# Hybrid decoder trunk on one core: one turn in each eighth chunk of the up-projection, mixer products back and forth from tile to tile, out-projection operands moved by 64 and 128 bytes

## The chip, the core and the metric

The kernel runs on one core of one Trainium2 chip. The metric is the device time of one execution in microseconds (us), lower is better; before the change three runs took 1076.39, 1076.42 and 1076.58 us, median 1076.42 us. One further execution was profiled. In what follows TensorE is PE, VectorE is DVE, ScalarE is ACT, GpSimd is POOL, and SP issues most of the transfers.

## What is computed

One decoder layer for 256 tokens of width 2048: a mixer that runs attention heads and a causal convolution side by side on one input projection, an output projection, and a gated MLP with a three-tap convolution. All in float32. Cut to what matters here:

```python
h = rms_norm(x, mix_norm_g[l])
proj = h @ w_in[l]
q, kv, gate_logits, conv_in = jnp.split(proj, splits, axis=-1)
...
attn = nsa_attention(q, kv, gates, rel_bias, cmp_pos[l], cmp_w1[l], cmp_w2[l])
conv = conformer_conv(conv_in, conv_w[l], conv_b[l], conv_ln_g[l], conv_ln_b[l])
x = x + jnp.concatenate([attn, conv], axis=-1) @ w_out[l]
h = rms_norm(x, ffn_norm_g[l])
x = x + conv_glu_ffn(h, w_up[l], ffn_conv_w[l], ffn_conv_b[l], w_down[l])
...
return rms_norm(x, final_norm_g)

def conv_glu_ffn(h, w_up, cw, cb, w_down):
    u = causal_depthwise_conv(h @ w_up, cw, cb)
    a, gate = jnp.split(u, 2, axis=-1)
    return (jax.nn.silu(gate) * a) @ w_down
```

`w_in` has 5680 columns, `w_up` 2 x 5632, `w_down` is 5632 x 2048. The four matrix products hold nearly all of the arithmetic.

## The kernel before

**Float32 in parts.** PE multiplies in the format fp32r, which keeps fewer bits than float32. So every operand is split into a high part (a rounded copy, made by ACT) and a low part (what is left, made by DVE or POOL), and a product x·w becomes three: high times high, high times low, low times high. The weights stream in chunks of 1 MB (`raw`, three buffers `wraw`); `w_split` makes `wh` and `wl` of each (three buffers each), two chunks ahead of PE. A weight buffer is free again when PE has used it.

**The stages,** in the order in which PE runs them:

- *The head*, to 24 us: the first three chunks of the mixer's projection, in pieces as their transfers land.
- *The mixer's projection*, to 250 us: 29 chunks through `tile_chunk` (L501). Each is one tile of 128 columns of `w_in` and 16 tiles of the sum over 2048, and each of the 16 goes through `mm3` (L252): three matmuls of 256 columns, with `wh` stationary twice and `wl` once. Between the chunks, and within them where `hook` says so, PE is given other matmuls: the compressed branch (`cmp_in`, L735), spreads of norms, the attention itself. After the 21st of the 29 chunks, six chunks for the values come with their own loops, then eight for the queries, with the attention's matmuls among them.
- *The out-projection*, to 353.5 us: `out_group` and `out_unit` (L1095, L1105), 125 calls of `mm_rows` (L269), each three matmuls of 512 columns. Here the activations are the stationary operand (`ma_h`, `ma_l` of the attention, `mc_h`, `mc_l` of the convolution, `ms_h`, `ms_l` of sums) and the weights stream.
- *The up-projection*, to 840 us: 88 chunks, numbered here 4m + 2·part + kh from 0 to 87 (loop at L1356). Each chunk has 16 steps j; a step is one `whole` (L1369: `wh` stationary, 512 columns, the high and the low activations side by side) and one `low` (L1381: `wl` stationary, 256 columns, the high activations). I call the two a pair. ACT and DVE work on the results meanwhile (`up_out`).
- *The down-projection*, to 1066 us, then the last norm and the stores.

**The order of the products.** PE takes its instructions in the order in which the program issues them, and two small tables set the order of matmuls that belong to one sum. They change no operand:

- `ROUNDS` (L49) orders the three products of `mm3`. It has four entries, taken in turn from chunk to chunk by `st["use"]`, and each entry has one order for every odd and one for every even call. Written with A for a matmul that has `wh` stationary and B for `wl`, two calls in a row are: order 0 AAB AAB, order 1 ABA ABA, order 2 BAA AAB, order 3 ABA AAB.
- `TURNS` (L50) orders steps 4 and 5 of an up-projection chunk, from chunk 4 on (`m > 0`), by the chunk's number modulo 5. Written with W for `whole` and L for `low`, the plain order of the two steps is W4 L4 W5 L5. Order 0 of the table is W4 L4 L5 W5, which I call the turn; 1 is W4 W5 L4 L5; 2 is the plain order; 3 is L4 L5 W4 W5; 4 is the plain order with W4 split into two matmuls of 256 columns (L1375). Chunks 0 to 3 are in plain order, but for other matmuls let into 0 and 1 (`between`).

**Where the tiles lie.** Tiles of one pool lie one behind the other in each partition's memory, so a longer tile moves all that follow it. In the built program the out-projection's stationary tiles `ma_h`, `ma_l`, `mc_h`, `mc_l`, `ms_h` all start 64 bytes past a multiple of 128, the high and the low parts alike. `wh` starts 64 bytes past such a multiple, `wl` and the activations `xt` on one.

Of the kernel before, what the change touches and what calls it, by code (L numbers as in the profile page):

```python
# [11 lines left out]
F32 = mybir.dt.float32  # L12
# [5 lines left out]
P = 128  # L18
T = 256
D = 2048  # L20
# [10 lines left out]
LINE = 16  # L31
# [12 lines left out]
CUTS = ((0, 1), (1, 2), (2, 4), (4, 5), (5, 6), (6, 8), (8, 10), (10, 12), (12, 14), (14, 16))  # L44
THIRD = {1: (0, 2), 2: (2, 4), 4: (4, 6), 5: (6, 8), 9: (8, 16)}
EARLY = 4


ROUNDS = (((0, 1, 2), (0, 1, 2)), ((0, 2, 1), (0, 2, 1)), ((0, 1, 2), (2, 1, 0)), ((0, 1, 2), (1, 2, 0)))  # L49
TURNS = (lambda w, s, l: ((w, 4), (l, 4), (l, 5), (w, 5)),  # L50
         lambda w, s, l: ((w, 4), (w, 5), (l, 4), (l, 5)),
         lambda w, s, l: ((w, 4), (l, 4), (w, 5), (l, 5)),
         lambda w, s, l: ((l, 4), (l, 5), (w, 4), (w, 5)),
         lambda w, s, l: ((s, 4), (l, 4), (w, 5), (l, 5)))


def head_of_slot(s):
# [5 lines left out]
def hybrid_trunk(ctx: ExitStack, tc: tile.TileContext, a: dict, out: bass.AP):  # L63
    nc = tc.nc
# [42 lines left out]
    st = {"dma": 3, "split": 3, "use": 0, "odd": 0}  # L107
# [4 lines left out]
    def w_dma():  # L112
        c = st["dma"]
        if c >= len(chunks):
            return
        st["dma"] += 1
        src, n = chunks[c]
        if c in kinds and c - down0 > 3 and (c - down0) % 4 == 3:
            raws[c] = late_pool[0].tile([P, CW], F32, name="wraw4", bufs=1)
        else:  # L120
            raws[c] = wpool.tile([P, CW], F32, name="wraw", bufs=NR)
        if c in far_sums:
            n = 1536
            nc.sync.dma_start(raws[c][:, n:], far_sums[c])
        if c == 4:
            nc.sync.dma_start(raws[c][:, :n // 2], src[:, :n // 2])
            halves.append(lambda: nc.sync.dma_start(raws[c][:, n // 2:], src[:, n // 2:]))
            return
        nc.sync.dma_start(raws[c][:, :n], src[:, :n])
# [101 lines left out]
    def w_next(cuts=1, ahead=LA):  # L231
        c = st["use"]
        st["use"] += 1
        w_pump()
        if st["split"] >= len(chunks):
            for f in lows:
                f()
            lows.clear()
        while st["split"] <= min(c + ahead, len(chunks) - 1):
            w_pump()  # L240
            w_split(cuts)
        if cuts == 1 or POOLED[0] <= st["split"] - 1 < POOLED[1]:
            w_pump()
        now = late[:]
        late.clear()
        if now:
            clock["dve"] = max(clock["dve"], clock["pe"])
        for f in now:
            f()
        return parts.pop(c)  # L250

    def mm3(ps, wh, wl, xh, xl, first, last):  # L252
        pairs = ((wh, xh), (wh, xl), (wl, xh))
        st["odd"] ^= 1
        for n, i in enumerate(ROUNDS[st["use"] % len(ROUNDS)][st["odd"]]):
            nc.tensor.matmul(ps, *pairs[i], start=first and n == 0, stop=last and n == 2)  # L256
        clock["pe"] += 0.36

    def mm_down(ps, xh, xl, wh, wl, first, last):
# [49 lines left out]
    xt_h, xt_l = [[xt[k // 4][:, k % 4, i] for k in range(KD)] for i in range(2)]  # L309


    with ExitStack() as mx:
        ap = mx.enter_context(tc.tile_pool(name="ap", bufs=1))
# [17 lines left out]

        ha = mixp.tile([P, KD + 8 * 512], F32, name="ha", tag="x2")
        raw2 = wpool.tile([P, CW], F32, name="wraw", bufs=NR)
        hb4 = [ap.tile([P, 4 * 512], F32, name=f"hb{i}", tag=tg) for i, tg in enumerate(("mah", "mal"))]
        mix_g = ha[:, :KD]
        heads, at = [], KD
        for n, (lo, hi) in enumerate(CUTS):
            w = 512 * (hi - lo)
# [6 lines left out]
                sl = slice(*[k * P for k in THIRD[n]])  # L345
                nc.sync.dma_start(raw2[:, sl], a["w_t"][0, :, sl])
        w_dma()
        xr = [ap.tile([P, D], F32, name=f"xr{t}", tag=tg) for t, tg in enumerate(("y", "us"))]
        nc.sync.dma_start(xr[0], x_rows[:, 0])
        w_dma()  # L350
        nc.sync.dma_start(xr[1], x_rows[:, 1])
# [24 lines left out]
        for n, ((lo, hi), (xc, *wc)) in enumerate(zip(CUTS, heads)):  # L376
            xs = [(xc[:, (k - lo) * T:(k - lo + 1) * T], k) for k in range(lo, hi)]
            sl = slice(lo * P, hi * P)
            if n < EARLY:
                h, l = parts[0]  # L380
# [49 lines left out]
        scratch = nc.dram_tensor("rel_scratch", (16, 384), F32, kind="Internal").ap()  # L430

        CU0 = P - 32
        alive = ap.tile([P, 4 * LINE], F32, name="alive")[:, :1]
        wb = mixp.tile([P, 16, T], F32, name="wb", tag="x2")

        def tab_neg():
# [64 lines left out]
        def tile_chunk(ps, ticks={}, half=None):  # L501

            wh, wl = w_next(2)
            held = pieces[:] if half else []
            del pieces[:len(held)]
            for kt in range(KD):
                if kt == KD // 2 and half:
                    half()
                    pieces.extend(held)
                if kt % 4 == 2:  # L510
                    hook(kt // 4, ticks)
                sl = slice(kt * P, (kt + 1) * P)
                mm3(ps, wh[:, sl], wl[:, sl], xt_h[kt], xt_l[kt], kt == 0, kt == KD - 1)
# [3 lines left out]
        y = ap.tile([P, 8, T], F32, name="y", tag="y")  # L517
# [49 lines left out]
        for j in range(8):  # L567
            gb, ab = [b[:, :T] for b in bank[2 * (j if j < 3 else (j + 1) % 2):][:2]]
            if j == 0:
                st["use"] = 3  # L570
                ps3 = gb, ab, bank[2][:, :T]
                for n, cut in enumerate(CUTS):
                    if n < EARLY:
                        for c, i, j in ((0, 0, 0), (0, 1, 0), (1, 0, 0), (0, 0, 1), (1, 0, 1), (1, 1, 0)):
                            for k in range(*cut):
                                nc.tensor.matmul(ps3[c], parts[c][i][:, k * P:(k + 1) * P], (xt_h, xt_l)[j][k],
                                                 start=k + i + j == 0, stop=False)
                                clock["pe"] += 0.12
                    for c, (lo, hi) in ((0, cut), (1, cut), (2, THIRD.get(n, (0, 0)))):
                        wh, wl = parts[c]  # L580
# [15 lines left out]
                first = gb, ab  # L596
# [3 lines left out]
            if j == 1:  # L600
                tok = ap.tile([P, 2, 5, P], F32, name="tok", tag="tok")
                nc.gpsimd.memset(tok[:, :, 4], 0.0)
                us = ap.tile([P, 8, PADT], F32, name="us", tag="us")
# [109 lines left out]
        for n in range(4):  # L713
            kv, i = divmod(n, 2)
# [111 lines left out]
        for kh in range(2):  # L826
            wh, wl = [w.rearrange("p (k c) -> p k c", c=256) for w in w_next(2)]
# [14 lines left out]
        for kq in range(4):  # L842
            wh, wl = [w[:, :4 * 304].rearrange("p (k c) -> p k c", c=304) for w in w_next(2)]
# [377 lines left out]
    with ExitStack() as fx:  # L1221
# [10 lines left out]
                                          ap=[[0, P], [1, D]]))  # L1232
# [8 lines left out]
        def g_load():  # L1241

            n = gn["n"]
            gn["n"] += 1
            if n >= NFT // 2:
                return
            q = n % (NFT // 4)
            gl = fw.tile([P, 8, P], F32R, name="gl", bufs=2)
            nc.gpsimd.dma_start(gl.bitcast(F32), gl_far[q])
            gq.append((gh_all[:, 4 * q:4 * q + 4].rearrange("p k a t -> p (k a) t"), gl))  # L1250
# [26 lines left out]
        def sum_steps():  # L1277

            for q in sums_todo[2::-1]:
                if len(q) == 3 and any(len(r) == 3 for r in sums_todo[:sums_todo.index(q)]):  # L1280
                    continue
                q.pop(0)()
            while sums_todo and not sums_todo[0]:
                sums_todo.pop(0)
# [58 lines left out]
        def up_stages():  # L1343
            for q in list(stages):
                q.pop(0)()
                if not q:
                    stages.remove(q)
# [8 lines left out]
        for m in range(NFT // 2):  # L1356
            ya = {}
            if m == NFT // 2 - 1:
                for _ in range(2):
                    g_load()  # L1360
            for part in range(2):
                bk = UP_BANKS[2 * ((2 * m + part) % 4):][:2]
                for kh in range(2):
                    wh, wl = [w.rearrange("p (k c) -> p k c", c=256) for w in w_next(1 if m + part + kh else 2)]
                    up_stages()
                    def whole(j):
                        k, i = divmod(j, 2)
                        kt = kh * 8 + k
                        nc.tensor.matmul(bk[i], wh[:, k, i * P:(i + 1) * P],  # L1369
                                         xt[kt // 4][:, kt % 4].rearrange("p a t -> p (a t)"), start=kt == 0, stop=False)  # L1370

                    def split(j):
                        k, i = divmod(j, 2)
                        for n, x in enumerate((xt_h, xt_l)):
                            nc.tensor.matmul(bk[i][:, n * T:(n + 1) * T], wh[:, k, i * P:(i + 1) * P], x[kh * 8 + k],  # L1375
                                             start=False, stop=False)

                    def low(j):
                        k, i = divmod(j, 2)
                        kt = kh * 8 + k  # L1380
                        nc.tensor.matmul(bk[i][:, :T], wl[:, k, i * P:(i + 1) * P], xt_h[kt], start=False, stop=kt == KD - 1)  # L1381

                    order = [(f, j) for j in range(16) for f in (whole, low)]
                    if m:
                        order[8:12] = TURNS[(4 * m + 2 * part + kh) % len(TURNS)](whole, split, low)
                    for f, j in order:
                        f(j)
                        if m + part == 0 and f is low and (kh, j) in between:
                            between.pop((kh, j))()
                up_out(m, part, bk, ya)  # L1390
                sum_steps()
# [267 lines left out]
```

## Time and profile before

| what | value |
|---|---|
| median of three runs | 1076.42 us |
| the profiled execution: its own time / its span | 1076.11 us / 1074.3 us |
| PE busy, share of the span | 1064.4 us, 99% |
| DVE busy, ACT busy, POOL busy | 898.0, 621.3, 366.8 us |
| PE instructions | 6738 matmuls |
| longest stages by PE's work: mixer's projection, out-projection, up-projection, down-projection | 24 to 250, 250 to 353.5, 353.5 to 840, 840 to 1066 us |
| last matmul starts | 1066.05 us |

How to read it: the span runs from the first to the last instruction of one profiled execution. The end of a matmul in the profile is modelled, and one starts before the one ahead of it has ended, so the busy time of a single matmul says little; what one costs is the distance from its start to the next start. The timeline view gives starts to 10 ns, and puts instructions with the same line and tiles that follow each other into one row with their count (x4).

### The profile page before, as it was taken

Reading aid. Unit: us, or ns where it says so; the run is one execution under the profiler, and the core shown is the slowest. Engines: PE = TensorE matmul, PEld = TensorE weight load, DVE = VectorE, ACT = ScalarE, POOL = GpSimd, SP = SyncE. Lnnn points to the kernel's source line nnn. Section 1 sums busy time; section 2 is a strip of 40 time slices with the busy share of each in tenths; the row PEclk is TensorE's granted clock in tenths of the full one; section 3 lists DMA queues with packets and bytes.
Section 4 is the critical chain, followed back from the end, with each engine's and each line's share of the span. In section 5 each row is a group of like instructions: output and inputs, shape, how many; then the busy total and the mean of one; then the engine's idle time right before and its main releaser. Section 6 shows DMA issues by size and latency. Waiting matters only on the chain.

```text
span 1074.3 us, 17561 instructions
## 1 busy us (share of the span) xinstructions
PE 1064.4 (99%) x6738; PEld 952.7 (89%) x6738; DVE 898.0 (84%) x1429; ACT 621.3 (58%) x895; POOL 366.8 (34%) x420
## 2 busy tenths in 40 slices
PE   9999999999999999999999999999999999999997
PEld 9999999998788888888888888888888888888886
DVE  7799987787895677778787878888787899999997
ACT  7544456778755555555555555555555555655563
POOL 0888976657000202224233434211121222211220
PEclk9999999999999999999999999999999999999999
DMA  9776756323556868999999999866678699979982
GB/s 355 245 264 255 209 158 237 119 80 118 196 198 217 272 231 262 276 290 284 300 279 302 280 302 307 278 214 223 222 234 282 216 385 348 350 283 344 327 314 97
DMA packets 62016, 272.82 MB, mean 254 GB/s; under 512 B 8187, under 2 KB 11531, under 8 KB 42348
## 3 DMA queue, kind: packets, MB, share of 16 engines
q1 hardware_dynamic: 34748, 199.33, 51.4%
q0 software_dynamic: 23536, 65.29, 22.6%
q10 hardware_dynamic: 3648, 7.08, 1.8%
q8 instruction: 53, 0.87, 0.3%
q14 instruction: 31, 0.25, 0.1%
HBM read 254.87 MB, written 41.18 MB: 276 GB/s over the span
## 4 chain that ended last, share of the span: by engine, by line
PE 95%; DVE 2%; DMA 1%; ACT 1%; issue 0%; SPq 0%; POOLq 0%; POOL 0%; DVEq 0%
PE bank L1369 30%; PE bank L1381 15%; PE bank L256 15%; PE bank L263 6%; PE bank L265 6%; PE bank L266 3%; PE bank L264 3%; PE bank L271 3%; PE bank L273 3%; PE bank L272 3%; PE bank L1024 1%; PE bank L1001 1%; DMA hb<-in_head 1%; PE bank L956 1%; PE bank L957 0%
## 5 line engine op out<-in xcount | busy, mean ns | idle before, releaser
L1369 PE MATMUL bank<-xt,wh 128*128 128x512 f32 x1391 | 474.9, 392 | 0.0
L215 ACT ACTIVATE wh<-wraw 128x1024 fp32r<-128x1024 f32 (+2 forms) x187 | 263.9, 1433 | 270.2 <-PE bank L1369 109.0
L1381 PE MATMUL bank<-xt,wl 128*128 128x256 f32 x1408 | 380.7, 278 | 0.0
L220 DVE TENSOR_TENSOR wl<-wraw,wh 128x2048 fp32r<-128x2048 f32 (+1 forms) x133 | 254.6, 1919 | 100.2 <-ACT wh L215 100.2
L1369 PEld LDWEIGHTS bank<-xt,wh 128*128 128x128 f32 x1391 | 257.7, 188 | 51.9
L1381 PEld LDWEIGHTS bank<-xt,wl 128*128 128x128 f32 x1408 | 263.2, 188 | 4.3
L256 PE MATMUL bank<-xt,wh 128*128 128x256 f32 x1004 | 177.2, 281 | 0.0
L256 PEld LDWEIGHTS bank<-xt,wh 128*128 128x128 f32 x1004 | 151.0, 188 | 0.8
L256 PE MATMUL bank<-xt,wl 128*128 128x256 f32 x502 | 132.6, 284 | 0.1
L220 POOL TENSOR_TENSOR wl<-wraw,wh 128x1024 fp32r<-128x1024 f32 (+1 forms) x54 | 122.4, 2319 | 17.3 <-ACT wh L215 17.3
L137 DVE TENSOR_TENSOR wl<-wraw,wh 128x2048 fp32r<-128x2048 f32 x44 | 100.4, 2286 | 4.4 <-ACT wh L136 4.3
L533 DVE SCALAR_TENSOR_TENSOR bank<-us,cw,bank 128x256 f32<-128x256 f32 x232 | 93.4, 483 | 0.7 <-ACT bank L528 0.3
L256 PEld LDWEIGHTS bank<-xt,wl 128*128 128x128 f32 x502 | 91.6, 188 | 1.7 <-issue 0.9
L1274 POOL DMA_DIRECT2D sum<-in_w_d x84 | 63.9, 859 | 73.2 <-issue 46.5
L136 ACT ACTIVATE xh<-sums 128x1536 fp32r<-128x1536 f32 x28 | 41.8, 1493 | 78.8 <-DVE sums L165 58.7
L136 ACT ACTIVATE wh<-wraw 128x2048 fp32r<-128x2048 f32 x44 | 82.9, 1904 | 7.3 <-PE bank L1369 3.8
L1308 DVE SCALAR_TENSOR_TENSOR yt<-u,fcw,yt 128x255 f32<-128x255 f32 (+1 forms) x176 | 80.9, 480 | 3.1
L1339 POOL DMA_DIRECT2D glf<-glt x22 | 12.9, 586 | 188.5 <-DVE glt L137 131.4
L265 PE MATMUL bank<-wl,gh 128*128 128x512 f32 x167 | 65.7, 393 | 0.0
L263 PE MATMUL bank<-wh,gh 128*128 128x512 f32 x167 | 65.6, 393 | 0.0
L992 POOL TENSOR_SCALAR e<-e,lsum 128x128 f32<-128x128 f32 x64 | 55.8, 888 | 22.8 <-ACT qs L879 14.7
L1256 POOL DMA_DIRECT2D gs<-gsf x56 | 30.6, 549 | 74.0 <-PE bank L266 71.9
(308 smaller groups left out, 1796.3 us busy)
## 6 DMA issues: line engine op xcount, KB each, us to landing
wraw<-in_w_u SPq DMA_DIRECT2D x88, 1024.0 KB, 7.2
wraw<-in_w_t SPq DMA_DIRECT2D x28, 1024.0 KB, 5.0
sum<-in_w_d POOLq DMA_DIRECT2D x84, 256.0 KB, 8.1
wraw<-in_w_d SPq DMA_DIRECT2D x28, 768.0 KB, 6.9
wraw<-in_w_d SPq DMA_DIRECT2D x16, 1024.0 KB, 7.0
gs<-gsf POOLq DMA_DIRECT2D x56, 256.0 KB, 6.6
wraw<-in_w_o SPq DMA_DIRECT2D x13, 1024.0 KB, 4.9
gl<-glf POOLq DMA_DIRECT2D x22, 512.0 KB, 5.8
```

The costliest lines, as they stand in the source:

```text
L136: nc.scalar.activation(hi, src, AF.Copy)
L137: return lambda: nc.vector.tensor_sub(lo, src, hi.bitcast(F32))
L215: nc.scalar.activation(h[:, sl], raw[:, sl], AF.Copy)
L220: (nc.gpsimd if pooled else nc.vector).tensor_sub(l[:, sl], raw[:, sl], h[:, sl].bitcast(F32))
L256: nc.tensor.matmul(ps, *pairs[i], start=first and n == 0, stop=last and n == 2)
L263: nc.tensor.matmul(ps, xh, wh, start=first, stop=False)
L265: nc.tensor.matmul(ps, xh, wl, start=False, stop=False)
L533: nc.vector.scalar_tensor_tensor(y[:, j] if last else acc[0], us[:, j, k:k + T], cw[:, j, k:k + 1], acc[0], op0=OP.mult, op1=OP.add)
L1274: sums_todo.append([lambda far=far, src=src, i=i: nc.gpsimd.dma_start(far, src[:, i * 512:(i + 1) * 512], **({"accum_op": OP.add} if i els ...
L1308: nc.vector.scalar_tensor_tensor(ys[i][:, d:], us_[i][:, :T - d], fcw[:, c, k:k + 1], ys[i][:, d:], op0=OP.mult, op1=OP.add)
L1369: nc.tensor.matmul(bk[i], wh[:, k, i * P:(i + 1) * P], xt[kt // 4][:, kt % 4].rearrange("p a t -> p (a t)"), start=kt == 0, stop=False)
L1381: nc.tensor.matmul(bk[i][:, :T], wl[:, k, i * P:(i + 1) * P], xt_h[kt], start=False, stop=kt == KD - 1)
```

## The change

Three edits.

1. `TURNS` is gone, and with it `split`. An up-projection chunk runs in plain order, but each chunk whose number modulo 8 is 2 (chunks 2, 10, 18, ..., 82) has the turn in steps 4 and 5.
2. `ROUNDS` is gone. Every call of `mm3` runs its three products forward or backward in alternation: the order 2 of the old table, in all chunks.
3. Four tiles get longer: `hb0` and `hb1` by 64 bytes, `xr0` by 128, `alive` by 64. `ma_l` then starts 64 bytes later, `y` 128 bytes later, `mc_h` and `ms_h` 256, `mc_l` 320; `ma_h` stays. `ma_l` and `mc_l` now start on a multiple of 128 bytes, `ma_h`, `mc_h` and `ms_h` still 64 past one. No instruction changes by this.

```diff
-ROUNDS = (((0, 1, 2), (0, 1, 2)), ((0, 2, 1), (0, 2, 1)), ((0, 1, 2), (2, 1, 0)), ((0, 1, 2), (1, 2, 0)))
-TURNS = (lambda w, s, l: ((w, 4), (l, 4), (l, 5), (w, 5)),
...
     def mm3(ps, wh, wl, xh, xl, first, last):
         pairs = ((wh, xh), (wh, xl), (wl, xh))
         st["odd"] ^= 1
-        for n, i in enumerate(ROUNDS[st["use"] % len(ROUNDS)][st["odd"]]):
-            nc.tensor.matmul(ps, *pairs[i], start=first and n == 0, stop=last and n == 2)
+        for n, pair in enumerate(pairs[::-1] if st["odd"] else pairs):
+            nc.tensor.matmul(ps, *pair, start=first and n == 0, stop=last and n == 2)
...
-        hb4 = [ap.tile([P, 4 * 512], F32, name=f"hb{i}", tag=tg) for i, tg in enumerate(("mah", "mal"))]
+        hb4 = [ap.tile([P, 4 * 512 + LINE], F32, name=f"hb{i}", tag=tg) for i, tg in enumerate(("mah", "mal"))]
...
-        xr = [ap.tile([P, D], F32, name=f"xr{t}", tag=tg) for t, tg in enumerate(("y", "us"))]
+        xr = [ap.tile([P, D + 2 * LINE * (1 - t)], F32, name=f"xr{t}", tag=tg)[:, :D] for t, tg in enumerate(("y", "us"))]
...
-        alive = ap.tile([P, 4 * LINE], F32, name="alive")[:, :1]
+        alive = ap.tile([P, 5 * LINE], F32, name="alive")[:, :1]
...
                     order = [(f, j) for j in range(16) for f in (whole, low)]
-                    if m:
-                        order[8:12] = TURNS[(4 * m + 2 * part + kh) % len(TURNS)](whole, split, low)
+                    if (4 * m + 2 * part + kh) % 8 == 2:
+                        order[10:12] = order[11:9:-1]
```

On PE, in steps 3 to 6 of up-projection chunk 8 (number 3 modulo 5, 0 modulo 8), the order before is this; `bank_66` and `bank_67` hold the two sums of the chunk, L1369 is `whole` and L1381 `low`:

```order
L1369 MATMUL bank_67<-xt,wh 128x512
L1381 MATMUL bank_67<-xt,wl 128x256
L1381 MATMUL bank_66<-xt,wl 128x256
L1381 MATMUL bank_67<-xt,wl 128x256
L1369 MATMUL bank_66<-xt,wh 128x512
L1369 MATMUL bank_67<-xt,wh 128x512
L1369 MATMUL bank_66<-xt,wh 128x512
```

After the change the same place of the same chunk reads as follows (the two lines are now L1361 and L1367):

```order
L1361 MATMUL bank_67<-xt,wh 128x512
L1367 MATMUL bank_67<-xt,wl 128x256
L1361 MATMUL bank_66<-xt,wh 128x512
L1367 MATMUL bank_66<-xt,wl 128x256
L1361 MATMUL bank_67<-xt,wh 128x512
```

The three `low` in a row and the three `whole` behind them have become alternating pairs, as in the rest of the chunk.

On PE at the start of the mixer's third gate chunk (order 3 of the old table, behind a chunk of order 2 that ends in `bank_69`), before:

```order
L256 MATMUL bank_69<-xt,wh 128x256 x4
L256 MATMUL bank_69<-xt,wl 128x256
L256 MATMUL bank_64<-xt,wh 128x256
L256 MATMUL bank_64<-xt,wl 128x256
L256 MATMUL bank_64<-xt,wh 128x256 x3
L256 MATMUL bank_64<-xt,wl 128x256
```

And after, at the same place:

```order
L248 MATMUL bank_69<-xt,wh 128x256 x4
L248 MATMUL bank_69<-xt,wl 128x256
L248 MATMUL bank_64<-xt,wl 128x256
L248 MATMUL bank_64<-xt,wh 128x256 x4
L248 MATMUL bank_64<-xt,wl 128x256 x2
```

The run of two `wl` and four `wh`, which stood in each fourth chunk, now goes on across the boundary and through all chunks. On DVE, ACT, POOL and SP no instruction moves; PE has 17 fewer, the second halves of the split `whole`.

More of the change, by code (lines that the diff above doesn't have):

```diff
@@ L46 @@
 EARLY = 4
-ROUNDS = (((0, 1, 2), (0, 1, 2)), ((0, 2, 1), (0, 2, 1)), ((0, 1, 2), (2, 1, 0)), ((0, 1, 2), (1, 2, 0)))
-TURNS = (lambda w, s, l: ((w, 4), (l, 4), (l, 5), (w, 5)),
[L51 to L54, printed above, removed]
 def head_of_slot(s):
@@ L1370, in whole @@
                                          xt[kt // 4][:, kt % 4].rearrange("p a t -> p (a t)"), start=kt == 0, stop=False)
[L1372 to L1376, printed above, removed]
                     def low(j):
```

## Prediction

> **What bounds the kernel now.** First the page, for the share of each engine and for the chain that ended last:
>
> ```profile
> span 1074.3 us, 17561 instructions
> PE 1064.4 (99%) x6738; PEld 952.7 (89%) x6738; DVE 898.0 (84%) x1429; ACT 621.3 (58%) x895; POOL 366.8 (34%) x420
> PEclk9999999999999999999999999999999999999999
> PE 95%; DVE 2%; DMA 1%; ACT 1%; issue 0%; SPq 0%; POOLq 0%; POOL 0%; DVEq 0%
> PE bank L1369 30%; PE bank L1381 15%; PE bank L256 15%; PE bank L263 6%; PE bank L265 6%; PE bank L266 3%; PE bank L264 3%; PE bank L271 3%; PE bank L273 3%; PE bank L272 3%; PE bank L1024 1%; PE bank L1001 1%; DMA hb<-in_head 1%; PE bank L956 1%; PE bank L957 0%
> ```
>
> PE is the chain, at full granted clock, and the two lines of the up-projection are 45% of it. Then the waits of PE, all that the view lists:
>
> ```profile
> PE bank L357 <- DVE ones L280: 1.0, 1, 1.0
> PE bank L956 <- DVE mn L966: 0.7, 1, 0.7
> ```
>
> 1.7 us in all, none of it behind the attention. So the time is the sum of the distances from one matmul's start to the next, and what the change can move is those distances. The third view is the timeline of PE, read by its starts. In the up-projection I look at the first matmul of chunks 2, 3, 4, 5, 6 and 10, of chunks 60 to 65 and 80, and at the first of the down-projection:
>
> ```profile
> 365.86 0.40 PE L1369 MATMUL bank<-xt,wh 128*128 128x512 f32 x1
> ...
> 371.46 0.40 PE L1369 MATMUL bank<-xt,wh 128*128 128x512 f32 x1
> ...
> 377.06 0.40 PE L1369 MATMUL bank<-xt,wh 128*128 128x512 f32 x1
> ...
> 382.56 0.39 PE L1369 MATMUL bank<-xt,wh 128*128 128x512 f32 x1
> ...
> 388.03 0.39 PE L1369 MATMUL bank<-xt,wh 128*128 128x512 f32 x1
> ...
> 410.10 0.40 PE L1369 MATMUL bank<-xt,wh 128*128 128x512 f32 x1
> ...
> 685.77 0.40 PE L1369 MATMUL bank<-xt,wh 128*128 128x512 f32 x1
> ...
> 687.17 0.40 PE L1369 MATMUL bank<-xt,wh 128*128 128x512 f32 x1
> ...
> 688.54 0.39 PE L1369 MATMUL bank<-xt,wh 128*128 128x512 f32 x1
> ...
> 688.88 0.39 PE L1369 MATMUL bank<-xt,wh 128*128 128x512 f32 x1
> ...
> 691.26 0.39 PE L1369 MATMUL bank<-xt,wh 128*128 128x512 f32 x1
> ...
> 696.74 0.39 PE L1369 MATMUL bank<-xt,wh 128*128 128x512 f32 x1
> ...
> 702.18 0.39 PE L1369 MATMUL bank<-xt,wh 128*128 128x512 f32 x1
> ...
> 707.73 0.40 PE L1369 MATMUL bank<-xt,wh 128*128 128x512 f32 x1
> 713.33 0.40 PE L1369 MATMUL bank<-xt,wh 128*128 128x512 f32 x1
> ...
> 796.03 0.40 PE L1369 MATMUL bank<-xt,wh 128*128 128x512 f32 x1
> ...
> 840.01 0.39 PE L263 MATMUL bank<-wh,gh 128*128 128x512 f32 x1
> ```
>
> This is the finding on which the rest stands. Chunks 2 and 3 run in plain order and take 5.60 us each (371.46 - 365.86, 377.06 - 371.46), which is 0.35 us a pair. Chunk 62 runs in the same plain order on the same sizes and takes 5.44 us (702.18 - 696.74), 0.34 us a pair. No engine waits in either. So a run of equal pairs has two paces, and keeps the one it is in: chunk 60 comes in at the slow one (four pairs from 685.77 to 687.17, 0.35 each), has the turn in steps 4 and 5, and goes on at the fast one (688.54 to 688.88). By order of the table the five chunks from 60 on take 5.49, 5.48, 5.44, 5.55 and 5.60 us, 27.56 together, 5.51 on average; from chunk 10 to chunk 80 it is 385.93 us for 70 chunks, 5.51 again, so this repeats. Order 3 throws the run into the slow pace, order 4 leaves it there, the turn brings it back.
>
> **The up-projection.** Removed: orders 1, 3 and 4 with their 17 extra matmuls. Kept: the turn, now in 11 chunks. Chunk 2 should be entered as now, at the slow pace, and be like chunk 60: 5.50. Ten later turns are entered at the fast pace. The trace has that once, chunk 5, 5.47 us (388.03 - 382.56), and it stayed fast. The other 75 chunks are plain, 5.44 if the pace holds. Chunk 2 to the end: 75 x 5.44 + 10 x 5.47 + 5.50 = 468.2 us, against 474.15 now (840.01 - 365.86). **Gain 6.0 us**, all on the path. Chunks 0 and 1 keep their order; I count 0, with 0.2 either way for the pace they are entered in. What must keep up is the supply of `wl`, which DVE makes two chunks ahead:
>
> ```profile
> 353.50:840.00 486.50, 486.50 (x2846) 429.44 (x2845) 387.38 (x519) 270.71 (x350) 132.89 (x191) 1.00 0.86 268
> ```
>
> In this stretch PE is busy throughout, DVE 387 of 486.5 us, ACT 271, the DMA engines 86%. With 480.5 us instead DVE is at 81%, the DMA at 87%. I cost the supply at nothing; if it fell behind, the wait would show on PE, and 6 us is all that could be lost.
>
> **The mixer's projection.** Its 29 chunks run 48 matmuls of 256 columns each. The starts of chunks of order 0, 1, 2 and 3 and of the next one, two sixes within the chunk of order 2, and two places where the same order 2 starts again behind other matmuls:
>
> ```profile
> 70.63 0.28 PE L256 MATMUL bank<-xt,wh 128*128 128x256 f32 x1
> ...
> 76.28 0.28 PE L256 MATMUL bank<-xt,wh 128*128 128x256 f32 x1
> ...
> 81.94 0.28 PE L256 MATMUL bank<-xt,wl 128*128 128x256 f32 x1
> 82.06 0.62 PE L256 MATMUL bank<-xt,wh 128*128 128x256 f32 x4
> ...
> 82.75 0.62 PE L256 MATMUL bank<-xt,wh 128*128 128x256 f32 x4
> ...
> 87.49 0.28 PE L256 MATMUL bank<-xt,wh 128*128 128x256 f32 x1
> ...
> 93.19 0.28 PE L256 MATMUL bank<-xt,wh 128*128 128x256 f32 x1
> ...
> 132.66 0.63 PE L256 MATMUL bank<-xt,wh 128*128 128x256 f32 x4
> ...
> 133.37 0.63 PE L256 MATMUL bank<-xt,wh 128*128 128x256 f32 x4
> ...
> 199.91 0.63 PE L256 MATMUL bank<-xt,wh 128*128 128x256 f32 x4
> ...
> 200.62 0.64 PE L256 MATMUL bank<-xt,wh 128*128 128x256 f32 x4
> ```
>
> The four orders take 5.65, 5.66, 5.55 and 5.70 us, 5.64 on average. After the change all are order 2. At 82 us it is the cheapest: six matmuls in 0.69 us (82.75 - 82.06), 5.52 to 5.55 a chunk. But there it is entered from a chunk of order 1. Where order 2 starts again behind other matmuls, six take 0.71 (133.37 - 132.66, and 200.62 - 199.91), which is 5.68 to 5.72 a chunk. So this order has two paces too, and with order 1 gone every stretch after the change starts in the second way. I take the slow one: 5.64 + 0.07 for the 21 chunks ahead of the values, **a loss of 1.4 us** (21 x 0.07), and nothing for the eight query chunks, which the attention's matmuls cut every few products now as then, nor for the head, whose products wait for transfers (`hb<-in_head` in the chain). At the fast pace instead it is a gain of 1.9 us in the 21 (0.09 each), 2.6 in all 29: the two ends.
>
> **The moved tiles.** The 125 calls of the out-projection are 375 matmuls of 512 columns with the moved tiles stationary. Two starts 30 matmuls apart:
>
> ```profile
> 323.18 0.39 PE L273 MATMUL bank<-wh,mc_l 128*128 128x512 f32 x1
> ...
> 330.14 0.39 PE L273 MATMUL bank<-wh,mc_l 128*128 128x512 f32 x1
> ```
>
> That is 0.232 us each. No run shows what the start of a stationary tile does, so the nearest rows bound it. The fast pair has 768 columns in 0.34 us, 0.227 for 512; the slow six of the mixer 1536 in 0.715, 0.238. So from -2.0 us (375 x 0.0053) to +2.4. I take 0: 0.232 lies in the middle, and nothing says which way. The few attention matmuls whose operands move lie within this.
>
> **The sum.** The profiled execution took 1076.11 us, its span 1074.3 and 1.8 around it. 1076.1 - 6.0 + 1.4 + 0 = 1071.5; the median of the runs is 0.3 above that execution, so **1071.8 us**. The down-projection is entered from a plain chunk at the fast pace, as now, and keeps its order and tiles: 0.
>
> **The rivals.**
>
> - *The mixer finds the fast pace.* From 65 to 127 us only projection matmuls run; if they lock as at 82 us, the mixer gains 1.9 instead of losing 1.4: 1068.5, and 1066.5 with the out-projection at its best end. For it: the chunk at 82 us does run so. Against: it lay behind order 1, and the two restarts quoted went slow. 0.22.
> - *A turn entered at the fast pace throws the run out.* Only chunk 5 speaks against it. Then chunk 10 goes slow, 18 fast, 26 slow: 35 plain chunks at 5.60 instead of 5.44 lose 5.6 us, nearly the whole gain, and with the mixer's loss it is 1077.4. 0.05.
> - *Slower: the fast pace does not hold without frequent turns.* Now plain pairs run fast for two chunks at most before order 3 ends it; after, for nearly eight. If something resets them, each plain chunk at 5.60 costs 0.16. The 4.6 us are gone at 29 slow chunks of 75, and from 43 on it is slower by what can be measured; with all 75 slow it is 1083.8. Against: the fast stretches last to the table's next disturbance in chunk after chunk, with the transfers and DVE of that place going on beside them. 0.05.
> - *The order is worth nothing.* With equal columns the up-projection, the mixer and the out-projection would stay as they are: 1076.4. The rows against it are 5.60 and 5.44 for one and the same order. 0.03. The Trainium skill has this rule: TensorE: Matmul & The Clock Gate, section Back-to-back issue gap, gives a matmul N / 2.4 GHz + 2.5 ns at full clock, by size alone. That is 0.325 us a pair (an estimate from that page), whatever stood before; the trace does not agree, with 0.34 and 0.35.
>
> **How the numbers follow.** The forecast has 0.65, and its own range is 1069.5 to 1074.4 by the out-projection's ends and chunks 0 and 1. A measurement of this kernel tells about 0.2%, 2.2 us, from no change. Faster by that: the forecast and the first rival, 0.87. Within it: the second, the fourth and part of the third, 0.09. Slower: 0.04. The range reaches to the first rival's better end and the forecast's worse end, 1066.5 to 1074.4, and leaves out about one in seven.
>
> **What would show it.** In the timeline after: each plain up-projection chunk 5.44 us, chunks with the turn 5.47, chunk 2 about 5.50, and the up-projection from chunk 2 on 468.2 us long. In the mixer six matmuls in 0.71 us between 65 and 127 us; 0.69 would make the first rival right. In the out-projection 0.232 us a matmul. The forecast is wrong if plain chunks of 5.60 stand behind a turn, if PE waits for `wl`, or if the mixer's and out-projection's sums leave their bounds.

## The result and the profile after

| | before | after |
|---|---|---|
| median of the runs of one comparison | 1076.50 us (1076.39 to 1076.94) | 1070.01 us (1069.72 to 1070.36) |
| the profiled execution: its own time / its span | 1076.11 / 1074.3 us | 1069.72 / 1067.9 us |

The ratio is 0.9939 (95% interval 0.9922 to 0.9956): faster, by 6.5 us or 0.6%. The forecast was 1071.8 us.

The head of the page after the change, and the waits of PE, answer to those of before:

```profile
span 1067.9 us, 17523 instructions
PE 1057.8 (99%) x6721; PEld 948.3 (89%) x6721; DVE 897.9 (84%) x1429; ACT 620.3 (58%) x895; POOL 368.2 (34%) x420
```

```profile
PE bank L349 <- DVE ones L272: 1.0, 1, 1.0
PE bank L948 <- DVE mn L958: 0.7, 1, 0.7
PE bank L248 <- DVE wl L359: 0.2, 1, 0.2
```

PE is still the chain; its busy time fell by 6.6 us with 17 matmuls fewer, and no wait for `wl` came up in the up-projection (the 0.2 us on L248 is in the head). So the time is again the sum of the distances from start to start. By stage, between the starts of their first matmuls, in us:

| | head | mixer, chunks 1 to 21 | values | query chunks | out-projection | up-projection | down-projection |
|---|---|---|---|---|---|---|---|
| before | 23.91 | 125.79 | 25.29 | 74.40 | 104.15 | 486.48 | 226.04 |
| after | 24.18 | 125.62 | 25.29 | 74.20 | 103.78 | 480.54 | 226.04 |
| difference | +0.27 | -0.17 | 0 | -0.20 | -0.37 | -5.94 | 0 |

The differences make -6.4 us, the difference of the two profiled executions. Nearly all of it is the up-projection. The timeline of PE after the change, first matmuls of chunks 2, 3, 4, 10, 11 and of the down-projection:

```profile
365.46 0.40 PE L1361 MATMUL bank<-xt,wh 128*128 128x512 f32 x1
...
370.96 0.39 PE L1361 MATMUL bank<-xt,wh 128*128 128x512 f32 x1
...
376.40 0.39 PE L1361 MATMUL bank<-xt,wh 128*128 128x512 f32 x1
...
409.04 0.39 PE L1361 MATMUL bank<-xt,wh 128*128 128x512 f32 x1
...
414.50 0.39 PE L1361 MATMUL bank<-xt,wh 128*128 128x512 f32 x1
...
833.62 0.39 PE L255 MATMUL bank<-wh,gh 128*128 128x512 f32 x1
```

Chunk 2, with the turn, takes 5.50 us, chunk 3, plain, 5.44, and chunk 10, with a turn entered at the fast pace, 5.46 to 5.47. From the records of all starts, each of the 75 plain chunks behind chunk 2 takes 5.44 us. The view by windows shows what works beside them:

```profile
353.08:833.62 480.54, 480.54 (x2829) 425.47 (x2828) 387.19 (x519) 270.30 (x350) 132.91 (x191) 1.00 0.87 272
```

The work of DVE and ACT is what it was (387 and 270 us) in 6 us less, and PE never stands still.

In the mixer I call two `wl` and four `wh` that follow each other a six. The timeline shows two sixes of chunk 1, and then three starts of the pair of `wl` that lies across a chunk's boundary, so that from one to the next there are eight sixes, a whole chunk:

```profile
24.30 0.62 PE L248 MATMUL bank<-xt,wh 128*128 128x256 f32 x4
...
24.99 0.62 PE L248 MATMUL bank<-xt,wh 128*128 128x256 f32 x4
...
87.58 0.40 PE L248 MATMUL bank<-xt,wl 128*128 128x256 f32 x2
...
93.23 0.40 PE L248 MATMUL bank<-xt,wl 128*128 128x256 f32 x2
...
98.88 0.40 PE L248 MATMUL bank<-xt,wl 128*128 128x256 f32 x2
```

A six takes 0.69 us in chunk 1; eight take 5.65 later (98.88 - 93.23), 0.706 each. 5.65 is neither the 5.55 nor the 5.70 to which the prediction gave its two cases. The first and last rows of the out-projection, 103.78 us apart:

```profile
249.30 0.39 PE L263 MATMUL bank<-wh,ma_h 128*128 128x512 f32 x1
...
353.08 0.40 PE L1361 MATMUL bank<-xt,wh 128*128 128x512 f32 x1
```

### The profile page after: what moved, and what is told of

Its sections match the earlier page's. It is cut to its first block, busy times and chain, and to the rows that moved or that the text cites. A ratio compares the mean times of both kernels' runs of the same rounds, so it can differ in the third digit from the quotient of the medians.

```text
span 1067.9 us, 17523 instructions
## 1 busy us (share of the span) xinstructions
PE 1057.8 (99%) x6721; PEld 948.3 (89%) x6721; DVE 897.9 (84%) x1429; ACT 620.3 (58%) x895; POOL 368.2 (34%) x420
## 4 chain that ended last, share of the span: by engine, by line
PE 95%; DVE 2%; DMA 1%; ACT 1%; issue 0%; SPq 0%; POOLq 0%; POOL 0%; DVEq 0%
PE bank L1361 30%; PE bank L248 15%; PE bank L1367 15%; PE bank L255 6%; PE bank L257 6%; PE bank L258 3%; PE bank L256 3%; PE bank L263 3%; PE bank L264 3%; PE bank L265 3%; PE bank L1016 1%; PE bank L993 1%; DMA hb<-in_head 1%; PE bank L948 1%; PE bank L949 0%
## 5 line engine op out<-in xcount | busy, mean ns | idle before, releaser
L1361 PE MATMUL bank<-xt,wh 128*128 128x512 f32 x1408 | 478.9, 389 | 0.0
L1367 PE MATMUL bank<-xt,wl 128*128 128x256 f32 x1408 | 387.1, 276 | 0.0
L1361 PEld LDWEIGHTS bank<-xt,wh 128*128 128x128 f32 x1408 | 263.5, 188 | 54.1
L1367 PEld LDWEIGHTS bank<-xt,wl 128*128 128x128 f32 x1408 | 264.3, 188 | 0.9
L248 PE MATMUL bank<-xt,wh 128*128 128x256 f32 x1004 | 158.7, 280 | 0.0
L248 PEld LDWEIGHTS bank<-xt,wh 128*128 128x128 f32 x1004 | 135.9, 188 | 0.4
L248 PE MATMUL bank<-xt,wl 128*128 128x256 f32 x502 | 108.5, 286 | 0.4 <-DVE wl L359 0.2
L248 PEld LDWEIGHTS bank<-xt,wl 128*128 128x128 f32 x502 | 79.3, 188 | 2.9 <-DVE wl L359 1.2
```

Source lines behind the costliest of these rows:

```text
L248: nc.tensor.matmul(ps, *pair, start=first and n == 0, stop=last and n == 2)
L1361: nc.tensor.matmul(bk[i], wh[:, k, i * P:(i + 1) * P], xt[kt // 4][:, kt % 4].rearrange("p a t -> p (a t)"), start=kt == 0, stop=False)
```

## The experiments

The theory: a run of equal pairs keeps its pace (the distance from start to start), and one turn is enough to change it. Its rivals are those of the prediction: the order is worth nothing; the pace fades without frequent turns; a turn entered at the fast pace throws it out. For the mixer and the tiles the experiments had to find a theory first. Each was compared with runs of the kernel before on the same chip, whose medians were 1076.34 to 1076.43 us. Stage times are worked out as in the table above.

### The up-projection: is it the turn, and how many?

**No turn at all.** The kernel after, with the condition and the exchange taken out:

```diff
-                    if (4 * m + 2 * part + kh) % 8 == 2:
-                        order[10:12] = order[11:9:-1]
```

> The changed kernel without any turn: all 88 up-projection chunks in plain order. Theory (a run of pairs keeps the pace it is in, and only the turn brings it back): chunk 1 ends slow, so chunks 2 to 87 take 5.60 us each, 481.6 us to the down-projection instead of 468.2, and the time is 1070.0 + 13.4 = 1083.4 us. Rival (the order is worth nothing, or the pace mends itself): 468 us less 11 turns of 0.03, time 1069.7.

Measured: 1083.66 us (1083.56 to 1083.81), ratio to before 1.0066 (1.0048 to 1.0084). First matmuls of chunks 2 and 3 and of the down-projection in its timeline:

```profile
366.11 0.40 PE L1361 MATMUL bank<-xt,wh 128*128 128x512 f32 x1
...
371.71 0.40 PE L1361 MATMUL bank<-xt,wh 128*128 128x512 f32 x1
...
847.71 0.40 PE L255 MATMUL bank<-wh,gh 128*128 128x512 f32 x1
```

All 86 chunks from 2 on take 5.60 us (481.6 together), against 468.16 after the change. Eleven exchanges of two matmuls are worth 13.4 us of 481.6. The granted clock was 0.998 in both profiled executions, so it is not what differs. The rival by which the order is worth nothing has fallen.

**One turn only, in chunk 2.**

```diff
-                    if (4 * m + 2 * part + kh) % 8 == 2:
+                    if 4 * m + 2 * part + kh == 2:
```

> The changed kernel with the turn in chunk 2 alone. Theory: the pace, once fast, holds for all 85 plain chunks behind it, 5.44 us each; the ten later turns cost 0.027 each and buy nothing, so 467.9 us from chunk 2 on and 1069.7 us. Rival (the fast pace does not hold for long, later turns renew it): plain chunks of 5.60 appear somewhere behind chunk 10, each 0.16 us; with half of them slow 1076.5.

Measured: 1070.07 us (1069.60 to 1070.52), ratio 0.9940 (0.9924 to 0.9955). First matmuls of chunk 3 and of the down-projection:

```profile
372.02 0.39 PE L1361 MATMUL bank<-xt,wh 128*128 128x512 f32 x1
...
834.42 0.39 PE L255 MATMUL bank<-wh,gh 128*128 128x512 f32 x1
```

462.40 us for 85 chunks is 5.44 each: the pace needs no renewal. The stage is 0.27 us shorter than after the change, 0.027 for each of the ten later turns, which are ballast. In the whole time that is lost in what the head and the first mixer chunks vary from execution to execution (the head was 23.6 to 24.9 us long in the profiles of this study). The rival by which the pace fades has fallen.

**The turn in chunk 2, and order 3 of the old table in chunk 46.**

```diff
-                    if (4 * m + 2 * part + kh) % 8 == 2:
+                    if 4 * m + 2 * part + kh == 2:
                         order[10:12] = order[11:9:-1]
+                    if 4 * m + 2 * part + kh == 46:
+                        order[8:12] = [(low, 4), (low, 5), (whole, 4), (whole, 5)]
```

> The changed kernel with the turn in chunk 2 alone and the old order 3 (L4 L5 W4 W5) in chunk 46 alone. Theory: chunks 3 to 45 take 5.44 us, 46 takes 5.55, 47 to 87 take 5.60 to the end, 6.6 us more than with one turn: about 1076.4 us; the down-projection, entered at the slow pace, shows whether its 226.0 us depend on that. Rival (pace set by what runs beside the matmuls): all chunks but 46 stay at 5.44, 1069.8.

Measured, in a single run: 1076.12 us. First matmuls of chunks 45, 46, 47 and 48, and of the down-projection:

```profile
599.37 0.39 PE L1361 MATMUL bank<-xt,wh 128*128 128x512 f32 x1
...
604.81 0.39 PE L1361 MATMUL bank<-xt,wh 128*128 128x512 f32 x1
...
610.37 0.40 PE L1361 MATMUL bank<-xt,wh 128*128 128x512 f32 x1
...
615.97 0.40 PE L1361 MATMUL bank<-xt,wh 128*128 128x512 f32 x1
...
839.97 0.40 PE L255 MATMUL bank<-wh,gh 128*128 128x512 f32 x1
```

5.44 us for chunk 45, 5.56 for chunk 46, 5.60 for chunk 47 and each behind it. One disturbance of four matmuls cost 6.7 us of the stage (486.95 against 480.28 with the turn alone). The down-projection, entered at the slow pace here, took 226.03 us: it doesn't take the pace over. With this the switch is shown in both directions: chunks 47 to 87 have the same order, sizes and neighbours as with the turn alone and differ in pace, so the pace is not set by what runs beside the matmuls. It also says what the removed table cost: it held both, the turn and order 3, in each five chunks.

**The up-projection's edit alone,** on the kernel before, with the old mixer orders and the old tiles:

```diff
-                    if m:
-                        order[8:12] = TURNS[(4 * m + 2 * part + kh) % len(TURNS)](whole, split, low)
+                    if (4 * m + 2 * part + kh) % 8 == 2:
+                        order[10:12] = order[11:9:-1]
```

> The kernel before with the up-projection's edit alone. Theory (the three edits act on separate stages): up-projection 480.5 us instead of 486.5 as in the changed kernel, the other stages as before: 1070.5 us, 0.5 above the changed kernel. Rival (part of the up-projection's gain needs the other edits, by the pace at which it is entered): a plain chunk of 5.60 or a time above 1071.

Measured: 1070.43 us (1069.98 to 1070.61), ratio 0.9943 (0.9927 to 0.9958). Chunk 2 and the end of the stage:

```profile
366.25 0.40 PE L1369 MATMUL bank<-xt,wh 128*128 128x512 f32 x1
...
834.42 0.39 PE L263 MATMUL bank<-wh,gh 128*128 128x512 f32 x1
```

468.17 us, as in the whole change: this edit makes the gain. For the other two edits 0.4 us is left between the medians of this kernel and of the whole change, which did not run side by side, and their ranges overlap.

### The tiles

**The old tile lengths** on the kernel after:

```diff
-        hb4 = [ap.tile([P, 4 * 512 + LINE], F32, name=f"hb{i}", tag=tg) for i, tg in enumerate(("mah", "mal"))]
+        hb4 = [ap.tile([P, 4 * 512], F32, name=f"hb{i}", tag=tg) for i, tg in enumerate(("mah", "mal"))]
...
-        xr = [ap.tile([P, D + 2 * LINE * (1 - t)], F32, name=f"xr{t}", tag=tg)[:, :D] for t, tg in enumerate(("y", "us"))]
+        xr = [ap.tile([P, D], F32, name=f"xr{t}", tag=tg) for t, tg in enumerate(("y", "us"))]
...
-        alive = ap.tile([P, 5 * LINE], F32, name="alive")[:, :1]
+        alive = ap.tile([P, 4 * LINE], F32, name="alive")[:, :1]
```

> The changed kernel with the four tiles at their old lengths. Theory (the start of the stationary tiles sets the out-projection's 0.4 us): from the end of the mixer's projection to the up-projection 104.15 us as before, not 103.78, all other stages as in the changed kernel, about 1070.4 us. Rival (the 0.4 us come from the order in which the mixer leaves PE): it stays at 103.78.

Measured, in a single run: 1070.90 us. The out-projection's first and last rows:

```profile
250.10 0.39 PE L263 MATMUL bank<-wh,ma_h 128*128 128x512 f32 x1
...
354.25 0.39 PE L1361 MATMUL bank<-xt,wh 128*128 128x512 f32 x1
```

104.15 us, as before the change. The three programs with the old lengths (this, the kernel before, the up-projection's edit alone) all have 104.15, the nine with the new ones 103.77 or 103.78, whatever their orders. So the tiles' place makes the 0.37 us, 1 ns on average for each of the 375 matmuls; the median distance behind a matmul with a low part stationary went from 231 to 229 ns, behind one with a high part it stayed at 232 to 233.

Two more stretches go with the lengths. The eight query chunks take 74.40 to 74.42 us in the three programs with the old ones, and 74.12 to 74.26 in eight of the nine with the new ones (74.37 in the ninth, whose alternation begins with the other call). Chunk 0 of the up-projection takes 6.37 us with the old and 6.42 with the new. By these stretches the edit is worth about 0.5 us in all.

Between this kernel and the one with the up-projection's edit alone lies nothing but the mixer's edit: 1070.90 us in one run here, 1069.98 to 1070.61 there. So no gain of the mixer's edit is shown.

**All stationary tiles on a multiple of 128 bytes:** the old lengths, and `w2`, which lies ahead of them, longer by 64 bytes.

```diff
-        w2 = ap.tile([P, HD], F32, name="w2")
+        w2 = ap.tile([P, HD + LINE], F32, name="w2")[:, :HD]
```

> The changed kernel with the old tile lengths, but one tile ahead of them 64 bytes longer, so that high and low parts of the out-projection's stationary operands all start on a multiple of 128 bytes. If it counts that high and low parts start at different places of 128 bytes, the out-projection is back at 104.15 us; if it counts that the low parts start on a multiple of 128, it is 103.78 or less. Other stages as in the changed kernel.

Measured, in a single run: 1070.72 us, and the out-projection 104.73 us: slower, not faster.

**The kernel after with `w2` longer by 64 bytes,** the same edit on the new lengths, so that the high parts start on such a multiple and the low parts 64 past one:

> The changed kernel with one tile ahead of the stationary tiles 64 bytes longer: high parts on a multiple of 128 bytes, low parts 64 past one, the mirror of the change. If it counts that high and low parts start at different places, the out-projection takes 103.8 us; if it counts where each starts by itself, something between 104.2 and 104.8, since with all on a multiple it was 104.73.

Measured, in a single run: 1070.24 us; the out-projection:

```profile
248.96 0.39 PE L263 MATMUL bank<-wh,ma_h 128*128 128x512 f32 x1
...
353.55 0.39 PE L1361 MATMUL bank<-xt,wh 128*128 128x512 f32 x1
```

104.59 us. With the start of the high and of the low parts past a multiple of 128 bytes written as a pair, the four are: (64, 64) 104.15, (64, 0) 103.78, (0, 0) 104.73, (0, 64) 104.59. That the parts lie differently is not what counts; the high parts do better at 64, and the low parts gain at 0 only then. The last two are one profiled execution each, all of these edits move tiles of the attention as well, and what larger distances (256, 512 bytes) do was not tried apart, so no rule is settled.

### The mixer

**Order 1 in chunks 3, 8 and 20,** on the thought that order 1, which stood ahead of the fast order 2 before, is the mixer's turn (`use` is the chunk's number here plus 3, for the three chunks of the head):

```diff
-        for n, pair in enumerate(pairs[::-1] if st["odd"] else pairs):
-            nc.tensor.matmul(ps, *pair, start=first and n == 0, stop=last and n == 2)
+        order = (0, 2, 1) if st["use"] in (6, 11, 23) else (2, 1, 0) if st["odd"] else (0, 1, 2)
+        for n, i in enumerate(order):
+            nc.tensor.matmul(ps, *pairs[i], start=first and n == 0, stop=last and n == 2)
```

> The changed kernel with the old order 1 (ABA ABA) in three mixer chunks: the fifth-numbered ones behind the three cuts, that is chunks 3, 8 and 20 of 29; all others order 2. Theory (order 1 is to the mixer what the turn is to the up-projection): the ten whole chunks between the second and the third cut take 5.55 us each instead of 5.65, and some of the four ahead of them, so 1.0 to 1.5 us less: 1068.7 us. Rival (the fast pace needs the whole old sequence 0, 1 ahead of it): they stay at 5.65, 1070.0.

Measured: 1070.02 us (1069.31 to 1070.64), ratio 0.9940 (0.9923 to 0.9956). Eight sixes of chunk 11 in its timeline:

```profile
82.56 0.63 PE L249 MATMUL bank<-xt,wh 128*128 128x256 f32 x4
...
88.27 0.63 PE L249 MATMUL bank<-xt,wh 128*128 128x256 f32 x4
```

5.71 us: behind order 1, chunks 10 to 18 went to the slowest pace. The theory fell.

**Order 0 in chunks 3, 8 and 20 and order 1 in the chunk behind each,** two steps of the old sequence (the line that sets `order`, the rest as in the kernel ahead):

```diff
+        order = (0, 1, 2) if st["use"] in (6, 11, 23) else (0, 2, 1) if st["use"] in (7, 12, 24) else (2, 1, 0) if st["odd"] else (0, 1, 2)
```

> As the run with order 1 in three chunks, but order 0 (AAB AAB) in those three and order 1 in the chunk behind each. Theory that order 1 is the turn and its entry does not count: chunks of order 2 behind it take 5.55 us, nine between the cuts, 1068.8 us. Rival (order 1 leads to the fast pace only from the pace that order 0 leaves, as in the kernel before): fast here and not in the run without order 0.

Measured: 1069.92 us (1069.58 to 1070.16), ratio 0.9941 (0.9926 to 0.9955). Chunks 5 and 6 took 5.55 us, chunks 11 to 18 took 5.71: the same sequence led to both ends. Inconclusive, but for this: the order of the last chunk alone does not decide.

**The alternation begun with the other call,** so that every chunk begins AAB instead of BAA and each cut falls three matmuls further on in the six:

```diff
-    st = {"dma": 3, "split": 3, "use": 0, "odd": 0}
+    st = {"dma": 3, "split": 3, "use": 0, "odd": 1}
```

> The changed kernel with the alternation in the mixer begun one call later: each chunk begins with A A B instead of B A A, so the same endless run of two B and four A is cut by the other matmuls at another place in its six. Theory (the pace of order 2 is settled at each cut, by where in the six it falls): the chunks between the second and the third cut, 5.65 us in all executions of the changed kernel but one form, take another of the paces seen, 5.55 or 5.71, all alike: 1 us less or 0.6 us more in the mixer. Rival (the place of the cut does not count): 5.65.

Measured: 1069.02 us (1068.74 to 1070.20), ratio 0.9934 (0.9919 to 0.9949). Eight sixes, from the last two matmuls of chunk 9 to the same place in chunk 10:

```profile
81.56 0.62 PE L248 MATMUL bank<-xt,wh 128*128 128x256 f32 x4
...
87.10 0.62 PE L248 MATMUL bank<-xt,wh 128*128 128x256 f32 x4
```

5.54 us: chunks 8 to 18 all run at the fastest pace, with the same order of products. What lies ahead of them is a cut at 63 us in chunk 7, two matmuls of the relative-bias table (`tab_rel`, L434); where it falls in the six is what was changed, from between the two `wl` to among the four `wh`, and the pace behind it changed from 5.65 to 5.55. The pace ahead of it doesn't explain this: here it was 5.71, and so it was in the runs with no turn and with one, which left the same cut at 5.65. This is one profiled execution; the run with the old tile lengths, where the cut is not moved, left it at 5.71 (see what stays open).

**Orders 3, 0 and 1 in chunks 3, 4, 5 and again in 8, 9, 10:** the whole way by which the kernel before came to its fast chunk at 82 us. Every other call stays as it was:

```diff
+        odd = st["odd"]
+        order = {6: (1, 2, 0) if odd else (0, 1, 2), 7: (0, 1, 2), 8: (0, 2, 1),
+                 11: (1, 2, 0) if odd else (0, 1, 2), 12: (0, 1, 2), 13: (0, 2, 1)}
+        for n, i in enumerate(order.get(st["use"], (2, 1, 0) if odd else (0, 1, 2))):
```

> The changed kernel with mixer chunks 3, 4, 5 and 8, 9, 10 of 29 in the old orders 3, 0, 1, all others order 2. Theory (order 2 runs fast only behind the pace that orders 3, 0, 1 in a row leave, as in the kernel before): chunks 11 to 18 take 5.55 us each instead of 5.65, and 6 and 7 too, about 1 us less in the mixer: 1069.0 us. Rival (it is chance at the cut ahead of it): 5.65 or 5.71 there.

Measured: 1068.86 us (1068.72 to 1069.12), ratio 0.9931 (0.9914 to 0.9947). Eight sixes from the start of chunk 11:

```profile
82.03 0.62 PE L251 MATMUL bank<-xt,wh 128*128 128x256 f32 x4
...
87.57 0.62 PE L251 MATMUL bank<-xt,wh 128*128 128x256 f32 x4
```

5.54 us, and so up to chunk 18. From two different programs, then, the plain alternation runs at 5.55 for eight chunks or more when it is brought there; in the second of them these chunks hold the same instructions as after the change, and only what lies ahead differs. The next kernel, with the same mixer, shows the same in its own execution.

**That mixer with one turn in chunk 2 of the up-projection,** the best of both:

> The two edits that the runs point to, together: mixer chunks 3, 4, 5 and 8, 9, 10 in the old orders 3, 0, 1 (all others order 2), and one turn in the up-projection, in chunk 2. Theory (the stages add up): 1068.9 less ten turns of 0.027, 1068.6 us; up-projection from chunk 2 on 467.9 us, mixer chunks 11 to 18 at 5.55. Rival (the time of the head, which differs by up to 1 us from run to run, hides so little): between 1068.2 and 1069.2.

Measured over five runs: 1068.69 us (1068.59 to 1069.17), ratio 0.9929 (0.9915 to 0.9942), against 1076.43 before on the same chip. It beats the kernel before by 7.7 us. Against the kernel after, which did not run beside it, it is 1.3 us faster by the medians, and the two ranges of times don't touch, though the intervals of the ratios overlap.

## Why the prediction was right, and where not

- **The up-projection: right, to the chunk.** Forecast 5.50 for chunk 2, 5.47 for the later turns, 5.44 for the plain chunks, 468.2 us from chunk 2 on and a gain of 6.0. Measured 5.50, 5.47, 5.44, 468.16 and 5.94; the 0.05 lies in chunk 0, within the 0.2 allowed, but it goes with the tiles and not with the pace of entry that the 0.2 was for. That the turn is the cause was an inference from one table that mixed five orders; the kernels with no turn, one turn and one throw show it. One reading beside it is too wide: PE waits for nothing in chunks 2, 3 and 62, but DVE and ACT do (DVE 4.8 us on `wh` in chunks 2 and 3); nothing hangs on it. On the rule weighed with the rival of no effect: the Trainium skill, TensorE: Matmul & The Clock Gate, section Back-to-back issue gap, gives N / 2.4 GHz + 2.5 ns as the gap of an isolated matmul, and about 131 ns at 512 columns for a stream of weight loads and matmuls. Neither figure depends on the order, and 5.60 against 5.44 us for the same matmuls agrees with neither.
- **The mixer: the step that failed.** It said that order 2 has two paces and that, with order 1 gone, every stretch starts in the slow one: "5.64 + 0.07 for the 21 chunks", a loss of 1.4 us. Measured: 125.62 us against 125.79. There are three paces: 5.547, 5.653 and 5.707 us a chunk (0.693, 0.707 and 0.713 a six), and from chunk 8 on the kernel after holds the middle one, 0.01 above the old average of 5.64. The two restarts were read rightly as slow: by the records of all starts both sixes took 0.713. What failed is the step from two short restarts behind other cuts to every stretch. The -0.17 us is no gain that the runs show either: in the seven profiled executions with these mixer orders the 21 chunks took 125.43 to 126.71 us, in the two with the old ones 125.79 and 126.52. The longest of the seven, with the old tile lengths, did run chunks 8 to 18 at the slow pace that was forecast; the other six held the middle one there. The query chunks, costed at nothing, took 0.20 us less, and that goes with the tiles. Not even the restarts kept their pace: after the change the first of them took 0.703 us by the records, and 0.706 for the next six:

```profile
132.83 0.63 PE L248 MATMUL bank<-xt,wh 128*128 128x256 f32 x4
...
133.53 0.63 PE L248 MATMUL bank<-xt,wh 128*128 128x256 f32 x4
```

- **The first rival, half right.** It had the mixer lock at the fast pace; it locked at a third one. The rival's mechanism exists, as the runs with the other alternation and with orders 3, 0 and 1 show at 1069.0 and 1068.9 us, near its 1068.5; the change did not reach it. In the number alone this rival lay nearer to the measured 1070.0 than the forecast's 1071.8 did.
- **The tiles: 0 taken, -0.37 measured** in the out-projection and -0.20 in the query chunks, within the bounds of -2.0 and +2.4. The place of 0 in the middle was a choice for want of a run, as the prediction says.
- **Head and supply.** The head was 0.27 us longer, within the 23.6 to 24.9 us that it took in the profiles of this study. `wl` kept up, and the down-projection stayed at 226.04 us, as assumed.

The forecast of the profiled execution was 1071.5 and it took 1069.7. The missing 1.8 us are the 21 mixer chunks' 1.6 (1.4 forecast, -0.17 measured) and the 0.57 that goes with the tiles (0.37 and 0.20), less the head's 0.27 and chunk 0's 0.05. The up-projection's term came out as worked out; the two smaller terms were off in the same direction, and the range was wide enough for them.

**What stays open.** Which place of a cut leads to which pace is not known: the same cut at 63 us gave the middle pace in the kernel after and in five others with its alternation (entered at the fast, middle and slow pace), but the slow one in the run with the old tile lengths, whose chunks ahead of the cut ran as in the kernel after. The tiles' place may act there too; one run can't say. What in PE keeps a pace was not shown by any run. A turn for the down-projection was not tried.

## What to carry to other kernels

When the bounding engine never waits, read distances from start to start and look for the same instructions in the same order at two distances: if there are two, the order of a few instructions somewhere ahead may hold a gain, and a kernel without them (here 5.60 against 5.44 a chunk) settles it in one run. In the up-projection here the pace stayed once it was entered, so count switches, not instructions: one that leads to the good pace, behind the last thing that disturbs it, was enough, and one stray disturbance cost all that followed. Read a pace over as long an unbroken stretch as the trace has, because a difference of 1% is less than the rounding of one short row, and don't carry it to a stretch that is entered in another way: the mixer's two restarts did not tell the pace of the long stretch.

## What the hardware showed that was not expected

- Alternating matmuls of 512 and 256 columns, PE never idle and the granted clock full, run at 0.340 or 0.350 us a pair, and kept either for as long as they went on: 85 chunks, 1360 pairs.
- Matmuls of 256 columns in the order AAB BAA ran at 115.6, 117.8 or 118.9 ns each (a chunk divided by 48). Moving a cut within the six, or other orders ahead, went with another of the three; which leads to which is open.
- The place of the stationary tiles, moved by 64 to 320 bytes, changed the out-projection between 103.78 and 104.73 us. The Trainium skill, SBUF — State Buffer, section Who interferes with whom, gives PE one read port for the moving operand and an independent one for weight loads, and counts contention only on the port that VectorE and GpSimd share; it says nothing of where a tile starts. These runs show that the start counts, and don't show why.
